# One slot block always, three conditional parts: the experts of a mixture-of-experts kernel cut anew

## The chip, the cores and the metric

The kernel runs on one core of a Trainium2 chip. The metric is the time of one execution on the device, in microseconds (us), as the median of several runs; a profile of one execution tells where it goes. The engines are TensorE (PE: matmuls, with a sequencer of its own, PEq, that reads the instructions; PEld is its loading of the stationary operand), VectorE (DVE), ScalarE (ACT), GpSimd (POOL), which here issues the gathers and scatters, and SyncE (SP), which issues the weights' transfers.

## What is computed

A decoder block for 512 tokens of width 1024: a state-space branch and a gated MLP branch, merged (the front of the kernel, 432 us), and then a mixture of experts, with which the change is concerned: each token goes to 4 of 32 experts, and each expert has a matrix of 1024 x 2048 for gate and up and one of 1024 x 1024 back.

```
logits = tok @ router_w + router_b
top_val, top_idx = lax.top_k(logits, 4); weights = softmax(top_val)
for e in range(32):                          # for the tokens that chose e
    gu = tok @ w_in[e] + b_in[e]             # 1024 -> 2048
    gate, up = min(gu[:, :1024], 7), clip(gu[:, 1024:], -7, 7)
    act = (up + 1) * (gate * sigmoid(1.702 * gate))
    out[tokens] += weight * (act @ w_out[e] + b_out[e])
x = x + gate2 * out; return rms_norm(x, final_g)
```

The inputs are fixed, and so is how many tokens come to each expert: between 12 and 159.

## The kernel before

**Slots.** An expert's tokens are put into slots, in steps of 32 (`SLOT`). Its weights are 12 tiles of 1 MB (8 `wi`, 4 `wo`), 384 in all, through a ring of 19 tiles in SBUF that SP's queue refills in the order of the experts, as far ahead as the ring lets it. The tokens' rows are gathered from DRAM by tables of slots (`tab0`, `tab1`, `tabp`) with an indirect DMA on POOL (`gather`, L1275), transposed on PE (L1298), and the results are added back into `acc` by an indirect DMA (`give`, L1383).

**Two shapes of block.** A block of 64 slots (`ab_up`, L1334, two halves u of 32 matmuls; `ab_out` and `ab_down`, L1343) puts 64 slots on the columns of the stationary operand and splits the 128 partitions of the result in 2. A block of 32 slots (`c_up`, L1366; `c_down`, L1376) splits them in 4, and takes as many matmuls as half a block of 64.

**What is unconditional.** In `expert(e)` a block of 64 slots always runs (tiles `xab`, PSUM tiles `pu` and `pd`, table `tab0`). Behind flat conditions, each an If on a flag that every engine has loaded from `nbt` (L1282), stand a single block of 32 (`single`, for 65 to 96 tokens and above 128) and a block of 64 more (`pair`, above 96). So an expert of up to 64 tokens takes two blocks of 32, one of 65 to 96 three, then four, then five.

**Order on PE.** It is the order of the code (PE is scheduled by hand): for each expert the flags' loads, the conditions of the gathers for e+2 (L1288, L1290; PE only steps past them), If single: up (L1434), If pair: up (L1436), the main block's up with the transposes of the next expert's rows between its halves, If single: down (L1445), If pair: down (L1447), the main block's down. All 32 experts are unrolled. A condition that is false makes an engine's sequencer jump over the rows of its body.

Of the kernel before, what the change touches and what calls it, by code (L numbers as in the profile page):

```python
# [29 lines left out]
SLOT = 32  # L30
# [11 lines left out]
def tile_hybrid_block(ctx: ExitStack, tc: tile.TileContext, x, c, ada_w, ada_b, norm1_g, w_in,  # L42
# [977 lines left out]
    reps = mc.tile([128, 5, 128], F32R, name="reps")  # L1020
    v.tensor_copy(reps[:, 0].rearrange("p (a b) -> p a b", a=2), ident[:, 0:64].unsqueeze(1).to_broadcast([128, 2, 64]))
# [3 lines left out]
    rep64, rep32 = [reps[:, 0]], [reps[:, 1 + j] for j in range(4)]  # L1025
# [106 lines left out]
    def positions(i, pps):  # L1132
        ns = slice(4 * i, 4 * i + 4)
        yield v.tensor_mul(pps_e, mk[:, i], pps[:, 0:32].unsqueeze(1).to_broadcast([128, 4, 32]))
        yield v.reduce_sum(pos[:, ns], pps_e, axis=mybir.AxisListType.X)
        yield one_hots(pos, 64, i)

    def later_hots(ch):

        v.tensor_scalar(pos2, pos, float(64 - 128 * ch), None, op0=OP.add)  # L1140
        for i in range(4):
            one_hots(pos2, 128, i)
# [52 lines left out]
    spread(slot_ps, 64, 1)  # L1195
    spread(slot_ps, 64, 2)
# [5 lines left out]
    spread(slot_ps, 64, 3)  # L1202
# [7 lines left out]
    tab0, tabp = [rt.tile([128, 1, 32, 3], I32, name=m) for m in ("tab0", "tabp")]  # L1210
    tab1 = rt.tile([128, 4, 32, 3], I32, name="tab1")
    tabl = dram.tile([18, 128, 96], I32, name="tabl")


    nbt = rt.tile([1, 97], I32, name="nbt")
    nbf = sm.tile([1, 97], F32, name="nbf")

    pair4 = rt.tile([128, 32], mybir.dt.uint8, name="pair4")
    def tables(t, n, reps, tab, mul, o, ps_, tile_):

        N = tab.shape[1]
        r = tile_("slt")[0:n]
        sc.activation(r, t[0:n, 0:96], AF.Copy)
        ps = ps_()
        for b, rep in enumerate(reps):
            pe.matmul(ps[:, 96 * b:96 * b + 96], rep[0:n], r, start=True, stop=True)
        pv = ps[:, 0:96 * N].rearrange("p (n v e) -> p n v e", n=N, v=3)
        iv, em = [tile_(n).rearrange("p (n e) -> p n e", e=32)[:, 0:N] for n in ("iv", "em")]
# [8 lines left out]
    def front_tile(n):  # L1237
        return sm.tile([128, 96], F32R, name=n) if n == "slt" else sm.tile([128, 64], F32, name=n)

    tables(slot_ps, 64, rep64, tab0, 2.0, 2, M, front_tile)  # L1240
# [6 lines left out]
    v.reduce_max(nbf[:, 96:97], nbf[:, 0:32], axis=mybir.AxisListType.X)  # L1247
    v.tensor_scalar(nbf[:, 64:96], cps[0:1, 0:32], 3.0 * SLOT + 0.5, None, op0=OP.is_gt)
    v.scalar_tensor_tensor(nbf[:, 32:64], cps[0:1, 0:32], 2.0 * SLOT + 0.5, nbf[:, 64:96], op0=OP.is_gt, op1=OP.subtract)
    v.scalar_tensor_tensor(nbf[:, 32:64], cps[0:1, 0:32], 4.0 * SLOT + 0.5, nbf[:, 32:64], op0=OP.is_gt, op1=OP.add)  # L1250
    v.tensor_copy(nbt, nbf)
    v.tensor_scalar(pair4, cps[:, 0:32], 3.0 * SLOT + 0.5, None, op0=OP.is_gt)
    later_hots(1)
    ordered.__exit__(None, None, None)
    xab = [rt.tile([128, 512], F32, name=f"xab{a}") for a in range(3)]
    xce = [rt.tile([128, 768], F32, name=f"xce{a}") for a in range(3)]
    gp.memset(xab[0], 0.0)
# [4 lines left out]
    pab = ctx.enter_context(tc.tile_pool(name="pab", bufs=1, space=PS, reuse_waits="tile"))  # L1262
    pcd = ctx.enter_context(tc.tile_pool(name="pcd", bufs=3, space=PS, reuse_waits="tile"))
# [15 lines left out]
    single, pair = {}, {}  # L1279

    def gather_first(e):
        single[e], pair[e] = [nc.values_load(nbt[0:1, o + e:o + e + 1], min_val=0, max_val=1) for o in (32, 64)]  # L1282
        gather(xab[e % 3], hrow2, tab0[:, 0, e, 0:1], 2)

    def gather_more(e):

        x_ = xce[e % 3]
        with tc.If(single[e] > 0):  # L1288
            gather(x_[:, 512:768], hrow4, tab1[:, 0, e, 0:1], 4)
        with tc.If(pair[e] > 0):  # L1290
# [287 lines left out]
```

## Time and profile before

| what | us |
|---|---|
| median of 3 runs | 1576.27 (1575.02 to 1578.70) |
| the profiled execution, its own time | 1573.51 |
| its span in the profile | 1571.9 |
| PE busy | 1397.8 (89%) |
| first expert's first up matmul | 432.5 |
| last expert's last matmul | 1544.1 |

The span is cut into the front (up to 432.5), the 32 experts (1111.6 us) and a tail of 27.8 us. "Idle before, releaser" in the profile's rows is the time for which an engine stood before the group of instructions, and what it waited for; PEq L1436 there means that PE's own sequencer came late, at the branch of line 1436.

### The profile page before, as it was taken

Reading aid. Unit: us, or ns where it says so; the run is one execution under the profiler, and the core shown is the slowest. Engines: PE = TensorE matmul, PEld = TensorE weight load, DVE = VectorE, ACT = ScalarE, POOL = GpSimd, SP = SyncE. Lnnn points to the kernel's source line nnn. Section 1 sums busy time; section 2 is a strip of 40 time slices with the busy share of each in tenths; the row PEclk is TensorE's granted clock in tenths of the full one; section 3 lists DMA queues with packets and bytes.
Section 4 is the critical chain, followed back from the end, with each engine's and each line's share of the span. In section 5 each row is a group of like instructions: output and inputs, shape, how many; then the busy total and the mean of one; then the engine's idle time right before and its main releaser. Section 6 shows DMA issues by size and latency. Waiting matters only on the chain. (4 is left out here: it accounts for less than half of the span.)

```text
span 1571.9 us, 21693 instructions
## 1 busy us (share of the span) xinstructions
PE 1397.8 (89%) x7671; PEld 643.2 (41%) x7672; DVE 519.3 (33%) x1095; ACT 345.4 (22%) x831; POOL 289.2 (18%) x204
## 2 busy tenths in 40 slices
PE   5889879969598889989999999998899999999992
PEld 3678757748432233323333333323233333333330
DVE  7868948893512111211111211111211111111114
ACT  3362313324321112111121112111121121211112
POOL 3643425350201010111010111101110211101001
PEclk9899979979699999999999999999999999999996
DMA  9353668383899999999997899989999999859953
GB/s 311 107 125 116 222 216 274 90 307 137 305 351 406 402 405 410 406 401 411 404 402 275 318 394 409 395 299 393 407 402 361 365 405 400 312 221 342 399 215 128
DMA packets 128915, 497.06 MB, mean 316 GB/s; under 512 B 23588, under 2 KB 31236, under 8 KB 95972
## 3 DMA queue, kind: packets, MB, share of 16 engines
q1 hardware_dynamic: 113844, 468.50, 76.3%
q0 software_dynamic: 11888, 20.84, 5.9%
q10 hardware_dynamic: 3008, 5.38, 1.0%
q8 instruction: 111, 1.82, 0.5%
q14 instruction: 64, 0.52, 0.1%
HBM read 476.75 MB, written 20.40 MB: 316 GB/s over the span
## 5 line engine op out<-in xcount | busy, mean ns | idle before, releaser
L1334 PE MATMUL pu<-wi,xab 128*64 128x512 f32 x2048 | 460.0, 602 | 1.8 <-issue 1.8
L1334 PEld LDWEIGHTS pu<-wi,xab 128*64 128x64 f32 x2048 | 144.8, 138 | 279.3 <-issue 269.1
L1343 PE MATMUL pd<-wo,aab 128*64 128x512 f32 x1024 | 233.8, 598 | 7.5 <-ACT aab L1306 7.3
L1304 ACT ACTIVATE xab<-pt,sh2c,g2c 128x64 f32<-128x64 f32 x304 | 93.8, 413 | 360.7 <-PE pt L1298 360.7
L1312 DVE TENSOR_SCALAR g<-pu 128x256 f32<-128x256 f32 x64 | 27.1, 423 | 405.3 <-PE pu L1334 401.2
L1343 PEld LDWEIGHTS pd<-wo,aab 128*64 128x64 f32 x1024 | 67.8, 136 | 129.1 <-issue 110.9
L1383 POOL DMA_INDIRECT acc<-yab,tab x32 | 50.7, 1585 | 361.4 <-DVE yab L1354 288.2
L175 POOL TENSOR_TENSOR wlo<-wraw,whi 128x1024 fp32r<-128x1024 f32 x34 | 93.0, 2738 | 128.0 <-ACT whi L174 114.7
L1275 POOL DMA_INDIRECT xab<-hrow,tab x32 | 33.6, 1051 | 375.7 <-PE pt L1298 373.1
L1366 PE MATMUL pc<-wi,xc 128*32 128x512 f32 x768 | 88.5, 608 | 9.6 <-DMA wi<-in_moe_w_in 6.8
L1354 DVE SCALAR_TENSOR_TENSOR yab<-pd,tab,gate2h 128x512 f32<-128x512 f32 x32 | 24.0, 751 | 199.9 <-PE pd L1343 199.9
L1313 ACT ACTIVATE s<-g 128x256 f32<-128x256 f32 x88 | 36.5, 415 | 222.2 <-DVE g L1312 220.6
L1334 PE MATMUL pc<-wi,xab 128*64 128x512 f32 x384 | 83.7, 594 | 1.0 <-ACT xab L1304 0.9
L403 PE MATMUL g<-hlo,whi 128*128 128x512 f32 x160 | 67.7, 423 | 7.1 <-DVE hlo L510 7.1
L403 PE MATMUL g<-hhi,whi 128*128 128x512 f32 x160 | 68.3, 427 | 2.7 <-ACT hhi L516 2.7
L1306 ACT ACTIVATE aab<-pt 128x256 f32<-128x256 f32 x64 | 24.5, 383 | 206.4 <-PE pt L1298 206.4
L1312 DVE TENSOR_SCALAR g<-pc 128x256 f32<-128x256 f32 x24 | 10.2, 424 | 170.4 <-PE pc L1366 96.6
L403 PE MATMUL g<-hhi,wlo 128*128 128x512 f32 x160 | 66.5, 415 | 0.0
L174 ACT ACTIVATE whi<-wraw 128x1024 fp32r<-128x1024 f32 x46 | 48.2, 1056 | 71.3 <-PE g L403 51.7
L354 DVE SCALAR_TENSOR_TENSOR adaw<-adaw,cT 128x1024 f32<-128x1024 f32 x28 | 54.4, 1944 | 0.8
L1298 PE MATMUL pt<-ident,act 128*128 128x128 f32 x176 | 36.3, 294 | 17.9 <-PEq L1447 10.4
L1298 PEld LDWEIGHTS pt<-ident,act 128*128 128x128 f32 x176 | 17.9, 141 | 80.9 <-issue 80.0
(446 smaller groups left out, 1644.8 us busy)
## 6 DMA issues: line engine op xcount, KB each, us to landing
wi<-in_moe_w_in SPq DMA_DIRECT2D x256, 1024.0 KB
wo<-in_moe_w_out SPq DMA_DIRECT2D x128, 1024.0 KB
adaw<-in_ada_w SPq DMA_DIRECT2D x16, 1024.0 KB
wraw<-in_w_in SPq DMA_DIRECT2D x12, 1024.0 KB
wraw<-in_ada_w SPq DMA_DIRECT2D x8, 1024.0 KB
wraw<-in_w_out SPq DMA_DIRECT2D x4, 1024.0 KB
xt<-in_x SPq DMA_DIRECT2D x4, 512.0 KB
wraw<-in_w_in SPq DMA_DIRECT2D x4, 512.0 KB
```

The lines of the kernel that those rows point to most:

```text
L174: sc.activation(dst_hi, src, AF.Copy)
L175: lo.tensor_sub(dst_lo, src, dst_hi)
L354: between.append(lambda k=k: v.scalar_tensor_tensor(a, w[k // 2][:, k % 2], cT[:, k:k + 1], a, op0=OP.mult, op1=OP.add))
L403: pe.matmul(P["ps"][m], l, r, start=(k == 0 and n == 0), stop=(k == 2 * P["n"] - 1 and n == 2))
L1298: pe.transpose(ps[:, 128 * j:128 * j + 128], src[:, 128 * j:128 * j + 128], ident)
L1304: sc.activation(t[:, o:o + w], ps[:, o:o + w], AF.Identity, scale=g2c[:, k:k + 1], bias=sh2c[:, k:k + 1])
L1312: v.tensor_scalar(g, p[:, 0:256], LIMIT, None, op0=OP.min)
L1313: sc.activation(sg, g, AF.Sigmoid, scale=ALPHA)
L1334: pe.matmul(p[u][64 * g:64 * g + 64, :].rearrange("p (a b) -> p a b", a=2), xT[:, k % 4, 64 * (k // 4):64 * (k // 4) + 64], wi[k][:, :, 51 ...
L1343: pe.matmul(p[64 * g:64 * g + 64, :], aT[:, k % 2, 16 * (k - k % 4):16 * (k - k % 4) + 64], wo[k // 2 + j][:, k % 2, 512 * g:512 * g + 512 ...
L1366: pe.matmul(p[32 * g:32 * g + 32, :].rearrange("p (a b) -> p a b", a=2), xT[:, k % 2, 32 * (k // 2):32 * (k // 2) + 32], wi[k][:, :, 256 * ...
L1383: gp.indirect_dma_start(out=rows_, out_offset=bass.IndirectOffsetOnAxis(ap=icol, axis=0), in_=y, in_offset=None, compute_op=OP.add)
```

## The change

The unconditional part of an expert becomes one block of 32 slots (`c_up` and `c_down`, PSUM tag `pm`, rows `xm`, table `tab0` for slots 0 to 31). Behind three flat Ifs stand a single block (33 to 64 tokens, and 97 to 128; `tab1`), a pair of 64 slots (above 64; `taba`) and a second pair (above 128; `tabb`). So an expert takes as many blocks of 32 as it needs, from one to five. The main block's up now stands behind the three conditional ups (but ahead of them for expert 0), and the next expert's transposes behind it. Each expert loads three flags. The gathers of conditional rows are issued one expert ahead instead of two, into two buffers (`xe`) instead of three. In the front, the first pass of one-hot tables goes to 96 slots instead of 64, two more tables are worked out on DVE there (`tab1` and `taba`), and two more small operations on the flags.

```diff
-    pair4 = rt.tile([128, 32], mybir.dt.uint8, name="pair4")
+    over3 = rt.tile([128, 32], mybir.dt.uint8, name="over3")
...
+    over = lambda n, dst, x_, op: v.scalar_tensor_tensor(dst, cps[0:1, 0:32], n * SLOT + 0.5, x_, op0=OP.is_gt, op1=op)
+    v.tensor_scalar(nbf[:, 64:96], cps[0:1, 0:32], 2.0 * SLOT + 0.5, None, op0=OP.is_gt)
+    v.tensor_scalar(nbf[:, 96:128], cps[0:1, 0:32], 4.0 * SLOT + 0.5, None, op0=OP.is_gt)
+    over(1.0, nbf[:, 32:64], nbf[:, 64:96], OP.subtract)
+    over(3.0, nbf[:, 32:64], nbf[:, 32:64], OP.add)
+    v.tensor_sub(nbf[:, 32:64], nbf[:, 32:64], nbf[:, 96:128])
     v.tensor_copy(nbt, nbf)
+    tables(slots, 96, rep32[1:2], tab1, 4.0, 0, M, front_tile)
+    tables(slots, 96, rep64[1:], taba, 2.0, 2, M, front_tile)
     later_hots(1)
...
     def gather_first(e):
-        single[e], pair[e] = [nc.values_load(nbt[0:1, o + e:o + e + 1], min_val=0, max_val=1) for o in (32, 64)]
-        gather(xab[e % 3], hrow2, tab0[:, 0, e, 0:1], 2)
+        flags[e] = [nc.values_load(nbt[0:1, o + e:o + e + 1], min_val=0, max_val=1) for o in (32, 64, 96)]
+        gather(xm[e % 3], hrow4, tab0[:, 0, e, 0:1], 4)
...
+    def pair_up(x_, wi, sel, n):
+        p, a_ = [PC(), PC()], acts(4, "actp", 2)
+        ab_up(transposed(x_, 4, "xab", 1, True), wi, sel, n, p)
+        return [swiglu(t, a) for t, a in zip(p, a_)]
+
+    def pair_down(a_, wo, sel, n, row):
+        lT = [transposed(t, 2, "ac", 4) for t in a_]
+        ab_out(PC(), lT[0], lT[1], wo, sel, n, row)
...
         if e + 2 < NE:
             gather_first(e + 2)
-            gather_more(e + 2)
-        act, last = acts(2, "act"), acts(3, "actc")
-        with tc.If(single[e] > 0):
-            c_up(transposed(x_[:, 512:768], 2, "xc", 2, True), wi, sel, n, last[2])
-        with tc.If(pair[e] > 0):
-            p = ab_up(transposed(x_[:, 0:512], 4, "xab", 2, True), wi, sel, n, [PC(), PC()])
...
-        nxt = []
-        p = ab_up(xT, wi, sel, n, [pab.tile([128, 512], F32, tag=f"pu{u}", name="pu") for u in range(2)],
-                  lambda: nxt.extend(start(e + 1) if e + 1 < NE else []))
...
+        if e and e + 1 < NE:
+            gather_more(e + 1)
+        (act,), (one,) = acts(1, "act"), acts(1, "actc")
+        ups = {}
+
+        def main_up():
+            c_up(xT, wi, sel, n, act, PM())
+
+        if e == 0:
+            main_up()
+        with tc.If(single > 0):
+            c_up(transposed(x_[:, 0:256], 2, "xm", 3, True), wi, sel, n, one)
+        with tc.If(pair > 0):
+            ups[0] = pair_up(x_[:, 256:768], wi, sel, n)
+        with tc.If(pair2 > 0):
+            ups[1] = pair_up(x_[:, 768:1280], wi, sel, n)
+        if e:
+            main_up()
+        nxt = start(e + 1) if e + 1 < NE else []
+        with tc.If(single > 0):
+            c_down(transposed(one, 2, "ac", 4), wo, sel, n, tab1[:, 0, e])
+        with tc.If(pair > 0):
+            pair_down(ups[0], wo, sel, n, taba[:, 0, e])
+        with tc.If(pair2 > 0):
+            pair_down(ups[1], wo, sel, n, tabb[:, 0, e])
+        c_down(transposed(act, 2, "am", 2), wo, sel, n, tab0[:, 0, e], PM())
```

On PE, the up part of one expert of the kernel before, from the first condition to the end of the main block's up (`pc` are the conditional blocks' PSUM tiles; "32x512 x32" is a block's matmuls, each of which the trace shows as two matmuls with two weight loads, and `xce` the gathered rows of the conditional blocks):

```order
L1434 COMPARE_AND_BRANCH
L1298 MATMUL pt<-ident,xce_3257 128x128 x2
L1366 MATMUL pc<-wi,xc 32x512 x32
L1434 UNCONDITIONAL_BRANCH x2
L1436 COMPARE_AND_BRANCH
L1298 MATMUL pt<-ident,xce_3257 128x128 x4
L1334 MATMUL pc<-wi,xab 64x512 x32
L1436 UNCONDITIONAL_BRANCH x2
L1334 MATMUL pu<-wi,xab 64x512 x16
L1298 MATMUL pt<-ident,xab_3252 128x128 x4
```

The same place in the changed kernel (line 1463 is the single's If, 1465 the pair's, 1467 the second pair's; `xe` holds the conditional rows, `xm` the main block's):

```order
L1463 COMPARE_AND_BRANCH
L1386 MATMUL pc<-wi,xm 32x512 x32
L1463 UNCONDITIONAL_BRANCH x2
L1465 COMPARE_AND_BRANCH
L1310 MATMUL pt<-ident,xe_3280 128x128 x4
L1344 MATMUL pc<-wi,xab 64x512 x32
L1465 UNCONDITIONAL_BRANCH x2
L1467 COMPARE_AND_BRANCH
L1467 UNCONDITIONAL_BRANCH x2
L1333 MATMUL pm<-bhl,sel 128x512
L1386 MATMUL pm<-wi,xm 32x512 x32
L1310 MATMUL pt<-ident,xm_3277 128x128 x2
```

A third conditional body, as long as the second, now stands between the loads and the main block's up, and what follows it is one block of 32 matmuls in the place of two halves of 16 in 64-slot form.

The down part of the changed kernel on the same engine, from the single's If (line 1472) past the pair's (1474) and the second pair's (1476) to the main block's down (`act` are the activations that are transposed):

```order
L1472 COMPARE_AND_BRANCH
L1396 MATMUL pc<-wo,ac 32x256 x32
L1474 COMPARE_AND_BRANCH
L1361 MATMUL pc<-wo,ac 64x512 x16
L1476 COMPARE_AND_BRANCH
L1310 MATMUL pt<-ident,act 128x128 x4
L1333 MATMUL pc<-bhl,sel 128x256 x2
L1476 UNCONDITIONAL_BRANCH x2
L1310 MATMUL pt<-ident,act 128x128 x2
L1333 MATMUL pm<-bhl,sel 128x256
L1396 MATMUL pm<-wo,am 32x256 x32
```

Here too a third condition with a body of 16 matmuls of 64x512 has come in, and the main block's down, 16 of 64x512 before, is 32 of 32x256.

## Rows read from the trace of the kernel before

**Rows 1.** The page: DMA share in 40 slices; the instruction queue's packets, MB.

```profile
DMA  9353668383899999999997899989999999859953
...
q8 instruction: 111, 1.82, 0.5%
```

**Rows 2.** Windows, experts 0 to 9 and 10 to 31.

```profile
core 0: us, PE busy (x) PEld busy (x) DVE busy (x) ACT busy (x) POOL busy (x), PEclk, DMA share, GB/s
432.50:739.70 307.20, 279.92 (x1481) 94.85 (x1480) 49.38 (x114) 51.64 (x152) 35.99 (x28) 0.97 1.01 399
739.70:1544.10 804.40, 763.80 (x4228) 266.44 (x4226) 136.39 (x317) 136.91 (x418) 90.08 (x67) 1.00 0.91 351
```

**Rows 3.** Windows, one expert of two, three, four and five blocks.

```profile
671.10:696.50 25.40, 23.65 (x111) 8.03 (x110) 4.38 (x10) 3.96 (x12) 3.91 (x3) 1.00 1.03 405
1419.90:1456.70 36.80, 35.43 (x244) 12.55 (x242) 6.46 (x15) 7.13 (x22) 3.14 (x2) 1.00 0.94 357
765.10:812.90 47.80, 46.53 (x219) 16.11 (x218) 8.06 (x19) 8.04 (x24) 4.25 (x3) 1.00 1.02 403
812.90:872.30 59.40, 58.27 (x351) 20.72 (x352) 10.15 (x24) 10.98 (x34) 5.76 (x4) 1.00 0.77 291
```

**Rows 4.** PE's groups, the single's and the pair's ups.

```profile
L1366 PE MATMUL pc<-wi,xc 128*32 128x512 f32 x768 | 88.5, 608 | 9.6 <-DMA wi<-in_moe_w_in 6.8 <-ACT xc L1304 2.8
L1334 PE MATMUL pc<-wi,xab 128*64 128x512 f32 x384 | 83.7, 594 | 1.0 <-ACT xab L1304 0.9
```

**Rows 5.** Timeline of PE in expert 28 (three blocks): start, length, work, idle before.

```profile
1420.76 7.07 PE L1366 MATMUL pc<-wi,xc 128*32 128x512 f32 x64 [0.23 <-ACT xc L1304]
...
1428.65 7.09 PE L1334 MATMUL pu<-wi,xab 128*64 128x512 f32 x32
...
1444.18 3.66 PE L1376 MATMUL pc<-wo,ac 128*32 128x256 f32 x64 [0.35 <-ACTq L1447]
...
1449.06 1.94 PE L1343 MATMUL pd<-wo,aab 128*64 128x512 f32 x8 [0.23 <-ACT aab L1306]
...
1451.30 5.37 PE L1343 MATMUL pd<-wo,aab 128*64 128x512 f32 x24
```

**Rows 6.** Timeline of PE after two conditions passed over, up and down.

```profile
671.72 0.70 PE L1321 MATMUL pu<-bhl,sel 128*128 128x512 f32 x2 [0.58 <-PEq L1436]
...
662.65 0.41 PE L1298 MATMUL pt<-ident,act 128*128 128x128 f32 x2 [0.73 <-PEq L1447]
```

**Rows 7.** Branches of the pair's conditions on PE's sequencer, ns min/median/max.

```profile
L1436 PEldq COMPARE_BRANCH  x38: 70/218/5188, 430.8 to 1519.6; - x38
...
L1447 PEldq COMPARE_BRANCH  x38: 70/213/437, 448.7 to 1535.0; - x38
```

**Rows 8.** Timeline of PE at the late entries of the main up.

```profile
580.67 0.70 PE L1321 MATMUL pu<-bhl,sel 128*128 128x512 f32 x2 [3.06 <-PEq L1436]
581.31 8.78 PE L1334 MATMUL pu<-wi,xab 128*64 128x512 f32 x32
...
1088.95 0.70 PE L1321 MATMUL pu<-bhl,sel 128*128 128x512 f32 x2 [3.43 <-PEq L1436]
1089.58 7.09 PE L1334 MATMUL pu<-wi,xab 128*64 128x512 f32 x32
```

**Rows 9.** Windows on the first half of the main up, behind two late entries.

```profile
581.30:590.00 8.70, 8.70 (x33) 2.61 (x32) 0.00 (x0) 0.00 (x0) 0.00 (x0) 0.80 1.05 389
...
1089.60:1096.70 7.10, 7.10 (x34) 2.29 (x34) 0.00 (x0) 0.00 (x0) 0.00 (x0) 1.00 1.04 381
```

**Rows 10.** Gathers of conditional rows on POOL (ns), and the gathers' landing.

```profile
L1275 POOL DMA_INDIRECT xce<-hrow,tab x12: 997/1075/1241, 486.0 to 1415.4; - x12
...
DMA to landing us min/median/max: 6.3/6.9/9.1
```

**Rows 11.** Timeline of DVE in the front: a table's first and last operation.

```profile
413.84 0.19 DVE L1229 TENSOR_SCALAR em<-m 128x32 f32<-128x32 f32 x1 [1.60 <-PE m L1226]
...
414.53 0.20 DVE L1235 TENSOR_TENSOR tab<-tab,m 128x32 f32<-128x32 f32 x1
```

More of the change, by code (lines that the diff above doesn't have):

```diff
@@ L1024, in tile_hybrid_block @@
                       ident[:, 32 * j:32 * j + 32].unsqueeze(1).to_broadcast([128, 4, 32]))
-    rep64, rep32 = [reps[:, 0]], [reps[:, 1 + j] for j in range(4)]
+    v.tensor_copy(reps[:, 5].rearrange("p (a b) -> p a b", a=2), ident[:, 0:64].unsqueeze(1).to_broadcast([128, 2, 64]))
+    rep64, rep32 = [reps[:, 5], reps[:, 0]], [reps[:, 1 + j] for j in range(4)]
     tok4 = sm.tile([128, 4], F32, name="tok4")
@@ L1237, in front_tile @@
     def front_tile(n):
-        return sm.tile([128, 96], F32R, name=n) if n == "slt" else sm.tile([128, 64], F32, name=n)
-    tables(slot_ps, 64, rep64, tab0, 2.0, 2, M, front_tile)
+        return sm.tile([128, 96], F32R, name=n) if n == "slt" else sm.tile([128, 32], F32, tag=n, name=n)
+    slots = sums(slot_ps, 96, front_tile)
+    tables(slots, 96, rep32[0:1], tab0, 4.0, 0, M, front_tile)
     cps = M()
@@ L1321, in biased, with acts, ab_up @@
         return pe.matmul(o, s_, bhl[:, n, cols_], start=first, stop=False)
-    def acts(n, tag):
-        return [mo.tile([128, 256], F32, tag=tag, bufs=n, name="act") for _ in range(n)]
-    def ab_up(xT, wi, sel, n, p, between=None):
+    def acts(n, tag, m=None):
+        return [mo.tile([128, 256], F32, tag=tag, bufs=n, name="act") for _ in range(m or n)]
+    def ab_up(xT, wi, sel, n, p):
         for u in range(2):
@@ L1330, in ab_up @@
         for k, u in [(k, u) for k in range(4) for u in range(2)] + [(k, u) for u in range(2) for k in range(4, 8)]:
-            if between and (k, u) == (4, 0):
-                between()
             for g in range(2):
@@ L1349, in ab_out @@
         ab_down(pd, aT0, 0, wo, (0, 1))
-        aT1 = aT1()
         ab_down(pd, aT0, 0, wo, (4, 5))
@@ L1359, in PC, with PM, c_up @@
         return pcd.tile([128, 512], F32, tag="pc", name="pc")
-    def c_up(xT, wi, sel, n, act):
-        p = PC()
+    def PM():
+        return pab.tile([128, 512], F32, tag="pm", name="pm")
+    def c_up(xT, wi, sel, n, act, p=None):
+        p = p or PC()
         biased(p, sel[:, 0], n, slice(0, 512))
@@ L1369, in c_up, with c_down @@
         return swiglu(p, act)
-    def c_down(aT, wo, sel, n, row):
-        p = PC()
+    def c_down(aT, wo, sel, n, row, p=None):
+        p = p or PC()
         biased(p[:, 0:256], sel[:, 0], n, slice(512, 768))
@@ L1403, in later_tables @@
         s_ = start(0) if ch == 1 else None
[L1404 to L1406 removed]
+        tab = mo.tile([128, 512], F32, tag="yab", bufs=2, name="tl")[:, 0:384].bitcast(I32)
+        tab = tab.rearrange("p (n e w) -> p n e w", n=4, w=3)
+        r = sums(t, 128, mo_tile)
+        tables(r, 128, rep32, tab, 4.0, 0, PT, mo_tile)
         if ch == 1:
[L1408 to L1411 removed]
+            tables(r, 128, rep64[0:1], tabb, 2.0, 2, PT, mo_tile)
+        gp.dma_start(tabl[4 * ch - 1:4 * ch + 3].rearrange("n p f -> p n f"), tab.rearrange("p n e w -> p n (e w)"))
+        return s_, tab
     ordered = tc.manual_schedule(engines={ET.PE})
     ordered.__enter__()
[L1415 to L1417 removed]
+    s_, tl = later_tables(1)
+    v.copy_predicated(tab1[:, 0], over3.unsqueeze(2).to_broadcast([128, 32, 3]), tl[:, 0])
+    most = nc.values_load(nbt[0:1, 128:129], min_val=0, max_val=NBMAX)
+    with tc.If(most > 7):
         for ch in (2, 3, 4):
```

103 lines of the change are left out of this document (40 added, 63 removed).

## The prediction, as it went on record

> **What bounds the kernel now.** I read the page first, then windows over the experts, PE's groups, PE's timeline within one expert, and last the branches. In the page the reader should see that DMA is full in most slices behind the front [rows 1]. The windows split that: to the end of expert 9 the queues are full (share 1.01), and PE works 280 of 307 us; from expert 10 on PE is busy 764 of 804 us and the queues are at 0.91 [rows 2]. So weights set the pace first, and PE afterwards. Second, an expert's time goes by its blocks: 25.4 us with up to two blocks of 32, 36.8 with three, 47.8 with four, 59.4 with five [rows 3]. There are 768/64 = 12 singles and 384/64 = 6 pairs [rows 4], which makes 17 experts of up to two blocks, 9 of three, 3 of four, 3 of five: 17 x 25.4 + 9 x 36.8 + 3 x 47.8 + 3 x 59.4 = 1085 us. The experts really take 1112; the other 27 us are waits for weights, late instructions and half-speed stretches behind them. How many of the 17 have one block only no trace shows; the reference's routing, counted on its inputs, gives 7 (experts 1, 2, 3, 5, 20, 23, 29) and 10 with two.
>
> Third, the late instructions. Two conditions passed over cost PE 0.58 us at the up and 0.73 at the down [rows 6]. The branch itself takes 0.2 us in the middle, but at the up's pair condition up to 5.19 us, at the down's never over 0.44 [rows 7]. A comparison of a register doesn't grow to 5 us; what it waits for is, I infer, the code behind it: the instruction queue brings 1.82 MB in 111 packets, 16.4 KB each [rows 1]. The difference between the places is the length of the jump. A single's up has 144 rows of instructions (64 matmuls, 64 weight loads, transposes, bias, semaphores, branches), a pair's up 150, the two downs 137 and 81. So a jump over 218 rows has always found its code there, one over up to 294 sometimes not. I take the middle, 256 rows, for a packet, and that PE's sequencer holds the packet it is in and asks for the next one when it enters it.
>
> **The change, part by part.**
>
> *Matmuls.* The main block's up falls from 2 x 7.09 to 7.07 us and its down from 1.94 + 5.37 to 3.66 [rows 5]: 10.8 us less. Back come one more passed condition at each end (some 0.2 us each) and a wait for the activations (four operations on DVE and ACT behind the last matmul, of which the first half's used to lie under the second half; I take 0.5 us, between 0 and 2). So a one-block expert needs 25.4 - 10.8 + 0.4 + 0.5 = 15.5 us. A single block more is 36.8 - 25.4 = 11.4 us and a pair 47.8 - 25.4 = 22.4 [rows 3], each less 0.5 for conditions no longer passed: 26.4, 37.4, 48.8 and 60 us for two to five blocks, where 25.4, 36.8, 47.8 and 59.4 stood. Ten experts lose 1 us, nine 0.6, six about 0.8, seven gain 9.9. In sum 1036: 49 us less than 1085 if nothing else waits.
>
> *Weights.* Experts 1, 2, 3 and 5 lie where the queues are full [rows 2]; their 40 us couldn't be had anyhow, since expert 9's last tiles come no sooner.
>
> *Code.* This is the term that decides. One expert's rows on PE, run or passed, are about 749 before (2.93 packets) and 1038 after (4.06; bodies of 144, 150, 152, 137, 81, 81 and the main block's 138 and 140). A one-block expert jumps over 446 rows at the up and 299 at the down, both beyond a packet; a two-block expert over 302 and 162. A packet's time F is at least 5.19 us [rows 7], and at most 25.4/2.93 = 8.7, the pace at which a two-block expert now gets through its packets; I take 5.5, near the row. Then I walk the rows of an expert: a packet can't be entered until F after the one before it. For one block: the jump of 446 rows takes 1 us, the main up 7.6, the jump of 299 about 1 and the down 5. If the first packet border lies at the expert's first row, the borders come at 0, 0.6, 4.6 and 9.2 us of undisturbed time; the second waits 4.9, the third 1.5, the fourth 0.9: 22.8 us. Borders 64, 128 and 192 rows later give 24.8, 23.9 and 21.9; the mean is 23.3, against 4.06 x 5.5 = 22.3 as the least. For two blocks (single up 8.3 us, jump 302 in 0.9, main up 7.8, down 4.5, jump 162 in 0.7, down 4) the four positions wait 1.5, 0.2, 5.3 and 6.6: 3.4 in the mean, 29.8. For three blocks no jump exceeds 152 rows and the walk gives 0.2 us: 37.6; for four and five nothing to 0.5. Bounds of this term: nothing (code always there), and F = 6.5 with 26.4 and 31.5 us.
>
> [...]
>
> *Clock.* [...] The walk has about 19 waits of over 3 us; three in four of them at 1.65 us make 23 us (bounds 0 and 31).
>
> *Small parts.* Two more tables at 0.9 us (five operations from 413.84 to 414.73 [rows 11]) and two flag operations stand on DVE ahead of the second one-hot pass: 2.2 us later for expert 0. The third flag's load and gather condition on PE's sequencer lie under its lead over PE; uncovered, 0.7 us an expert. The gathers are issued on POOL behind the previous expert's scatter, some 5 us into an expert; with 1.1 us and 6.9 to landing [rows 10] the conditional rows are there after 13 to 16 us, hidden under any expert of 22. Uncovered, 1 us in a few one-block experts. Issues of weights only follow PE.
>
> *Sum.* 7 x 23.3 + 10 x 29.8 + 9 x 37.6 + 3 x 48.8 + 3 x 60.3 = 1127; with the clock 1150, with the front's 2 us 1152, against 1112: +41 us. The weights no longer hold it up, since experts 0 to 9 would take 3 x 29.8 + 4 x 23.3 + 3 x 37.6 and their share of the clock, some 307 us as now. On the profiled 1573.5 that is 1614; the median lies 2.8 above this execution, so 1617. The walk leaves no room for waits at an expert's ends, and I go up to 1620.
>
> **Rivals.**
>
> *Code is always there in time* (chance 0.13). If F were under some 3.8 us (15.5/4.06), or two packets were held ahead, no jump would wait. For it: half of the branches at L1436 take 0.22 us or less, and none at L1447 over 0.44 [rows 7]. Against it: 5.19 us has been seen. Then experts 10 to 31 gain 3 x 9.9 less 7 x 1.0 and 12 x 0.7, that is 14 us; experts 0 to 9 gain the 7 us by which the main block's up behind the last tile is shorter; 2 us are lost in the front, and a few by gathers and by weights behind a short expert: about 1557 on the profiled execution and 1560 as a median, faster.
>
> *It evens out* (0.08). At F near 4.2 a one-block expert takes some 20 us and a two-block one 27.5; that gives back what the 14 + 7 us bring: 1576.
>
> *Longer waits* (0.13). F at 6.5 and the clock at half behind each wait: one-block experts 28, two-block 33, three-block 39: 196 + 330 + 351 + 148 + 184 = 1209, or +97: 1670. For it: the queues stay nearly full [rows 1], and F's upper bound is 8.7. Against it: the half-speed stretch failed to come once in the rows shown [rows 8].
>
> *The likeliest* (0.66): 1620, its own range 1585 to 1655.
>
> **How the numbers follow.** Faster is the first rival; same (within 0.2%, 3 us, about what a measurement of this kernel can tell) most of the second; slower the rest: 0.14, 0.06, 0.80. The range from 1564 to 1660 leaves out most of the first rival and of the third.
>
> **What would show it.** In the profile after: branches of the up's pair conditions at 3 to 6 us in nearly every one-block expert, and also at the down, where now none is over 0.44; more packets in the instruction queue, about 111 + 32 x 1.13 = 147; one-block experts of 21 to 28 us and two-block ones of 28 to 34; three-block experts within 2 us of 37.6; DMA share well under 1 also before 740 us; many stretches at a granted clock of 0.8 or less behind such waits. The prediction is wrong if the branches stay at 0.2 to 0.4 us, or if one-block experts come near 16 us.

## The result, and the profile after

The changed kernel takes 1684.72 us in the median (1681.11 to 1690.10, 4 runs), the kernel before in the same session 1575.64 us: ratio 1.069, 95% interval 1.0666 to 1.0714. It is slower, as forecast, but by 109 us where 44 were forecast, and outside the range. The profiled execution spans 1683.0 us, 111 more than before. The first up matmul comes 3.9 us later (436.5), the experts take 1219.7 us instead of 1111.6, and the tail is 1 us shorter.

The page of the changed kernel (busy time by engine, DMA share in 40 slices, the instruction queue's packets and MB):

```profile
PE 1362.1 (81%) x9935; PEld 654.8 (39%) x9936; DVE 514.5 (31%) x1093; ACT 359.3 (21%) x921; POOL 327.0 (19%) x229
...
DMA  9362757555499999999767899689995998856973
...
q8 instruction: 147, 2.41, 0.6%
```

and its windows over experts 0 to 9 and 10 to 31, then one expert of one, two, three, four and five blocks:

```profile
436.50:773.00 336.50, 252.15 (x2066) 92.57 (x2065) 43.04 (x101) 50.38 (x166) 41.22 (x31) 0.88 0.96 380
773.00:1656.20 883.20, 756.41 (x5906) 280.53 (x5906) 135.22 (x315) 150.92 (x492) 121.65 (x89) 0.96 0.82 315
1180.60:1210.70 30.10, 17.42 (x135) 6.01 (x134) 2.60 (x6) 2.94 (x10) 3.69 (x3) 0.72 1.03 405
1210.80:1245.20 34.40, 26.95 (x268) 10.24 (x268) 4.55 (x11) 5.90 (x20) 6.58 (x5) 0.90 1.02 398
1371.20:1410.90 39.70, 35.19 (x242) 12.80 (x242) 6.57 (x15) 6.91 (x22) 6.43 (x5) 1.00 0.93 371
803.60:853.10 49.50, 46.70 (x380) 17.52 (x376) 8.53 (x20) 9.75 (x32) 7.85 (x6) 1.00 0.80 312
853.10:917.20 64.10, 59.62 (x352) 21.48 (x350) 10.43 (x24) 10.76 (x34) 7.25 (x6) 0.97 0.59 214
```

Beside [rows 2] the reader sees PE doing less (1008.6 us busy in the experts instead of 1043.7) in a longer time, at a lower granted clock (0.88 and 0.96 instead of 0.97 and 1.00): PE stands idle for 211 us instead of 68. Beside [rows 3], the three-block expert shown takes 39.7 instead of 36.8 us, the four-block one 49.5 instead of 47.8, the five-block one 64.1 instead of 59.4. From the end of one main down to the next, the means over all experts of a size are 27.7, 31.9, 40.7, 49.5 and 64.1 us for one to five blocks; the one-block experts, which have 10.8 us less of matmuls, take longer than before (27.7 where the same seven took 26.4).

Where PE waits in an expert of one block (expert 20) and in one of two (expert 21), on its timeline:

```profile
1190.12 0.77 PE L1333 MATMUL pm<-bhl,sel 128*128 128x512 f32 x1 [9.48 <-PEq L1467]
1190.82 9.55 PE L1386 MATMUL pm<-wi,xm 128*32 128x512 f32 x64
...
1203.68 0.69 PE L1310 MATMUL pt<-ident,act 128*128 128x128 f32 x2 [2.94 <-ACTq L1476]
...
1204.84 5.94 PE L1396 MATMUL pm<-wo,am 128*32 128x256 f32 x64 [0.26 <-ACT am L1318]
...
1223.36 0.76 PE L1333 MATMUL pm<-bhl,sel 128*128 128x512 f32 x1 [3.75 <-PEq L1467]
1224.06 8.30 PE L1386 MATMUL pm<-wi,xm 128*32 128x512 f32 x64
...
1238.97 0.41 PE L1310 MATMUL pt<-ident,act 128*128 128x128 f32 x2 [1.82 <-DVEq L1474]
...
1239.85 5.35 PE L1396 MATMUL pm<-wo,am 128*32 128x256 f32 x64 [0.35 <-ACT am L1318]
```

The main up waits 9.48 us behind a jump over all three conditional ups, and 3.75 behind one over two of them. Both times the up that follows, 7.07 us at a granted clock of 1.00, takes 9.55 and 8.30 (granted 0.74 and 0.85), and the downs 5.94 and 5.35 instead of 3.66 (0.61 and 0.68). The branches themselves (lines 1465 and 1467, pair and second pair at the up; 1476, second pair at the down), and PE's longest waits over all experts:

```profile
L1465 PEldq COMPARE_BRANCH  x47: 70/176/4599, 451.9 to 1635.3; - x47
L1467 PEldq COMPARE_BRANCH  x35: 78/339/5650, 454.6 to 1638.0; - x35
L1476 PEldq COMPARE_BRANCH  x35: 73/217/3227, 461.2 to 1651.1; - x35
```

```profile
PE pm L1333 <- PEq L1467: 82.5, 28, 11.3
PE pt L1310 <- ACT xm L1316: 20.2, 18, 1.8
PE pt L1310 <- ACTq L1476: 18.9, 6, 3.4
PE pt L1310 <- PEq L1463: 17.1, 12, 1.7
PE pt L1310 <- PEq L1476: 12.4, 16, 4.2
...
PE pt L1310 <- DVEq L1474: 8.8, 6, 1.9
PE pc L1396 <- ACTq L1474: 8.6, 4, 2.6
PE pt L1310 <- ACTq L1472: 8.1, 3, 2.7
```

That a late branch waits for code can be read from the single packets in the trace. Each of the 20 branches of PE after 436 us that take over 0.7 us ends 1.3 to 1.5 us after a packet of the instruction queue has landed, and so do all 6 in the kernel before. In expert 20 packets land at 1182.92 and 1188.43, and the two late branches end at 1184.32 (L1465) and 1189.95 (L1467). Behind 16 of the 20 the next packet's transfer starts 3.0 to 3.6 us after the branch has ended, and it takes about 1.0: 3.3 + 1.0 + 1.4 = 5.7 us from one packet to the next.

So three places wait: the main up behind the jumps (82.5 us), the first transposes or matmuls of the downs (the rows at ACT xm, L1472, L1474 and L1476, together 77 us, 12.4 of them at PE's own branch L1476), and the first transposes of an expert (L1463, 17 us, and some 11 more under other names). Whatever the releaser, PE's idle time in the experts went from 26 to 82 us ahead of the main ups, from 30 to 95 ahead of the downs, and from 12 to 34 at the experts' starts. There is no wait for weights any more.

What stands ahead of the downs differs by expert. First ScalarE in expert 25 (three blocks), then VectorE in expert 21:

```profile
1395.70 0.38 ACT L1316 ACTIVATE xm<-pt,sh2c,g2c 128x32 f32<-128x32 f32 x1 [7.05 <-PE pt L1310]
...
1396.29 1.98 ACT L1316 ACTIVATE xm<-pt,sh2c,g2c 128x32 f32<-128x32 f32 x7
1398.12 0.42 ACT L1318 ACTIVATE ac<-pt 128x256 f32<-128x256 f32 x1
```

```profile
1237.21 0.48 DVE L1399 SCALAR_TENSOR_TENSOR yc<-pc,tab,gate2q 128x256 f32<-128x256 f32 x1 [4.36 <-PE pc L1396]
1237.62 0.41 DVE L1326 TENSOR_SCALAR u<-pm 128x256 f32<-128x256 f32 x1
...
1238.40 0.42 DVE L1328 SCALAR_TENSOR_TENSOR act<-u,g 128x256 f32<-128x256 f32 x1
```

In expert 25 the eight copies of the next expert's rows (`xm`) stand ahead of the first `ac` copy, which the pair's down needs, and PE waits 1.82 us there. In expert 21 it is no copy: the main block's activation (L1326 to L1328) stands on VectorE behind the result of the single's down (L1399), and the main down waits for it.

A last view, PE's groups, sizes the clock: 2048 main up matmuls (32 experts) and 2048 main down ones, and the pairs' downs (18 of them).

```profile
L1386 PE MATMUL pm<-wi,xm 128*32 128x512 f32 x2048 | 249.8, 643 | 0.0
...
L1396 PE MATMUL pm<-wo,am 128*32 128x256 f32 x2048 | 132.7, 416 | 11.1 <-ACT am L1318 10.8
L1361 PE MATMUL pc<-wo,ac 128*64 128x512 f32 x576 | 138.9, 639 | 0.1
```

At a granted clock of 1.00 these would be 32 x 7.07 = 226, 32 x 3.66 = 117 and 18 x 7.09 = 128 us: 50 us were lost there at 0.50, the lower of the two levels that the granted clock has in both traces, 24 of them in the main ups. In the experts the granted clock stood at that level in 29 stretches, 155 us in all; in the kernel before in 5, 23 us.

### The profile page after: what moved, and what is told of

Same layout as the page of the kernel before. It is cut to its first block, busy times and chain, and to the rows that moved or that the text cites. A ratio compares the mean times of both kernels' runs of the same rounds, so it can differ in the third digit from the quotient of the medians.

```text
span 1683.0 us, 27511 instructions
## 1 busy us (share of the span) xinstructions
PE 1362.1 (81%) x9935; PEld 654.8 (39%) x9936; DVE 514.5 (31%) x1093; ACT 359.3 (21%) x921; POOL 327.0 (19%) x229
## 4 chain that ended last, share of the span: by engine, by line
issue 26%; DMA 24%; another core or an unknown queue 1%; DVE 1%; POOLq 1%; PE 0%; POOL 0%; ACT 0%; ACTq 0%; DVEq 0%; SPq 0%
DMA acc<-yc,tab 14%; DMA acc<-yab,taba 5%; DMA acc<-yab,tabb 3%; DMA xe<-hrow,tab 2%; POOL xm L1284 0%; PE pm L1386 0%; POOLq L1292 0%; DMA fin<-acc 0%; DVE fs L1536 0%; DVE fs L1535 0%; DVE fin L1545 0%; POOLq L1403 0%; DVE fin L1552 0%; DVE fs L1537 0%
## 5 line engine op out<-in xcount | busy, mean ns | idle before, releaser
L1344 PE MATMUL pc<-wi,xab 128*64 128x512 f32 x1152 | 251.2, 594 | 2.0 <-ACT xab L1316 1.7
L1386 PE MATMUL pm<-wi,xm 128*32 128x512 f32 x2048 | 249.8, 643 | 0.0
L1316 ACT ACTIVATE xm<-pt,sh2c,g2c 128x32 f32<-128x32 f32 x360 | 104.6, 388 | 337.3 <-PE pt L1310 311.7
L1403 POOL DMA_INDIRECT acc<-yc,tab x45 | 73.0, 1623 | 505.1 <-DVE yc L1399 244.3
L1344 PEld LDWEIGHTS pc<-wi,xab 128*64 128x64 f32 x1152 | 81.2, 137 | 164.1 <-issue 149.0
L1396 PE MATMUL pm<-wo,am 128*32 128x256 f32 x2048 | 132.7, 416 | 11.1 <-ACT am L1318 10.8
L1361 PE MATMUL pc<-wo,ac 128*64 128x512 f32 x576 | 138.9, 639 | 0.1
L1386 PEld LDWEIGHTS pm<-wi,xm 128*32 128x32 f32 x2048 | 66.4, 117 | 164.2 <-issue 157.2
L1333 PE MATMUL pm<-bhl,sel 128*128 128x512 f32 x64 | 30.2, 471 | 88.7 <-PEq L1467 82.5
L1396 PEld LDWEIGHTS pm<-wo,am 128*32 128x32 f32 x2048 | 70.6, 119 | 64.3 <-ACT am L1318 17.1
L1386 PE MATMUL pc<-wi,xm 128*32 128x512 f32 x832 | 92.0, 594 | 3.5 <-ACT xm L1316 3.5
```

Of the source, the lines that this page charges most:

```text
L1316: sc.activation(t[:, o:o + w], ps[:, o:o + w], AF.Identity, scale=g2c[:, k:k + 1], bias=sh2c[:, k:k + 1])
L1344: pe.matmul(p[u][64 * g:64 * g + 64, :].rearrange("p (a b) -> p a b", a=2), xT[:, k % 4, 64 * (k // 4):64 * (k // 4) + 64], wi[k][:, :, 51 ...
L1361: pe.matmul(p[64 * g:64 * g + 64, :], aT[:, k % 2, 16 * (k - k % 4):16 * (k - k % 4) + 64], wo[k // 2 + j][:, k % 2, 512 * g:512 * g + 512 ...
L1386: pe.matmul(p[32 * g:32 * g + 32, :].rearrange("p (a b) -> p a b", a=2), xT[:, k % 2, 32 * (k // 2):32 * (k // 2) + 32], wi[k][:, :, 256 * ...
L1396: pe.matmul(p[32 * g:32 * g + 32, 0:256], aT[:, k % 2, 32 * (k // 2):32 * (k // 2) + 32], wo[k // 2][:, k % 2, 256 * g:256 * g + 256], sta ...
L1403: gp.indirect_dma_start(out=rows_, out_offset=bass.IndirectOffsetOnAxis(ap=icol, axis=0), in_=y, in_offset=None, compute_op=OP.add)
```

## Experiments

Three theories stood. *Code*: PE waits for rows of code behind long jumps. *Copies*: the eight copies of the next expert's rows, which the change had put between the main up and the downs on ScalarE, hold up the downs. *Sequencer*: three loads and three conditions at an expert's start are longer than PE's lead. All class means below are of the time from one expert's last main down matmul to the next's, read from each run's timeline.

**Code, by itself: a body that never runs, in the kernel before** (e4_before_pad, e5_before_pad_small). Both take the kernel before and add one condition at the up that is never true; its body has some 140 rows of PE in the one, one matmul in the other.

```diff
...
+        with tc.If(pair[e] > 1):
+            ab_up(xT, wi, sel, n, [PC(), PC()])
         nxt = []
```

```diff
...
+        with tc.If(pair[e] > 1):
+            biased(PC(), sel[:, 1], n, slice(0, 512))
         nxt = []
```

> The kernel before with a third condition at the up that is never true, with a body of 64 + 64 matmul and weight load rows on TensorE (about 140 rows) behind it. Theory 'code': the jump of the 17 experts that pass both conditions grows from 294 to some 435 rows; they wait 3 to 6 us more at the up, and half-speed stretches follow: 60 to 100 us more, about 1640 to 1675 us. Rival 'the condition itself' (the branch, the drain before it, the semaphores of the path passed): 0.2 to 0.4 us for each of 32 experts, about 10 us more, 1585 us.

> The kernel before with the same condition that is never true, but a body of one matmul. Theory 'code': the jump hardly grows, so only the condition's own price shows: 0.2 to 0.4 us for each of 32 experts, about 10 us more, 1585 us, far below the long body's time. Rival 'the condition itself': the same time as with the long body.

Measured: 1640.45 us with the long body (ratio 1.0391, 1.0327 to 1.0455), 1590.38 with the short one (1.0074, 1.0054 to 1.0094). Both came as the theory of code had it, the long body at the lower end of its range: the condition costs 12 us, 140 rows that never run cost another 50 (41 and 59 in the two runs of the long body). The 17 experts of up to two blocks rose from 25.9 us in the mean to 28.3 with the long body and 26.8 with the short one, so by less than the 3 to 6 us that were expected; the nine experts with a single alone rose as well (39.8 against 38.4). The new branch (ns, min/median/max), first long, then short, shows the wait itself:

```profile
L1440 PEldq COMPARE_BRANCH  x32: 208/399/3336, 435.9 to 1578.5; - x32
```

```profile
L1440 PEldq COMPARE_BRANCH  x32: 208/212/342, 435.6 to 1536.3; - x32
```

In e4 each branch of over 0.7 us ends 1.3 to 1.5 us after a packet has landed, as in the changed kernel. The instruction queue brings 129 packets with the long body and 112 with the short one: 17 more, as 32 x 138 rows at the prediction's 256 to a packet give.

**Code taken away again** (e10_no_pair2). The kernel e7 below without the second pair's bodies, so without the work of the slots from 128 on.

```diff
-        with tc.If(pair2 > 0):
-            ups[1] = pair_up(x_[:, 768:1280], wi, sel, n)
...
-        with tc.If(pair2 > 0):
-            pair_down(ups[1], wo, sel, n, tabb[:, 0, e])
```

> The kernel with fixed order and early rows (1655 us) without the second pair's ups and downs: 152 rows of code less at the up and 81 at the down of each expert. It leaves out the work of the slots from 128 on, in three experts of 32. Theory 'code': the jump of a one-block expert is 294 and 218 rows, that of a two-block expert 150 and 81, as in the kernel before: one-block experts 17 to 20 us instead of 25.9, two-block 27 to 28 instead of 32.6, five-block experts 38.5 as they now have three blocks: 7 x 7 + 10 x 5 + 3 x 23 = 168 us less, about 1487 us. Rival 'not the code': only the work left out goes, 3 x 23 and 0.3 us for two conditions less in each of the others, about 1570 us.

Measured: 1535.95 us (ratio 0.9742), 119 less than e7, between the two forecasts. One-block experts fell from 25.9 to 23.0 us, with 19.6 to 23.4 in six of them; two-block ones from 32.6 to 28.8, with 26.8 to 27.1 in five; the three experts that lost work went to 37.5. What the theory of code missed is the weights' queue: expert 3 took 32.0 and expert 24 took 37.1 us, with waits for weights of 7.3 and 5.8 us in them.

```profile
PE pt L1310 <- PEq L1465: 32.7, 16, 7.1
...
PE pc L1386 <- DMA wi<-in_moe_w_in: 10.3, 8, 2.2
```

Part of what the shorter code gives back is so taken by the weights. With three pairs of some 23 us, the work left out, it would stand at about 1605 us, still above the kernel before.

**Nested conditions** (e2_nested): one If on more than 32 tokens around the three, the second pair within the first.

```diff
...
+        with tc.If(nb[e] > 1):
+            with tc.If(single > 0):
+                c_up(transposed(x_[:, 0:256], 2, "xm", 3, True), wi, sel, n, one)
+            with tc.If(pair > 0):
+                ups[0] = pair_up(x_[:, 256:768], wi, sel, n)
+                with tc.If(nb[e] > 4):
+                    ups[1] = pair_up(x_[:, 768:1280], wi, sel, n)
...
```

> The changed kernel with its conditions nested: an outer If on more than 32 tokens around all three, the second pair inside the first pair's If; same bodies, so the same rows of code, and as many loaded flags. Theory 'each packet on the way': a wait comes for every packet of code in which a branch lies; one long jump lands in its target's packet at once, so a one-block expert waits for one packet per jump instead of up to two (5 to 6 us at the up instead of 7 to 11), 2 to 4 us at the up and up to 1 at the down less, and the passed conditions cost less: one-block experts 23 to 25 us instead of 27.7, two-block experts unchanged within 1 us: about 1655 us. Rival 'the code streams through whatever is jumped over': only the conditions' own price goes, 0.3 us each: about 1675 us.

Measured: 1721.72 us (ratio 1.0923, 1.0880 to 1.0967), slower than either theory. The one-block experts did go from 27.7 to 25.5 us, and the branch of their one jump waits up to 6.57 us:

```profile
L1464 PEldq COMPARE_BRANCH  x32: 65/70/6565, 445.3 to 1654.8; - x32
```

but all others lost (33.1, 42.2, 53.6, 64.5), at the downs: the edit had changed the order into which the scheduler puts ScalarE's work. In expert 15, for one, the single's `ac` copy stood ahead of all eight `xm` copies in the changed kernel and stands behind them here. That order hadn't been held still, so this run doesn't judge the total.

**Copies** (e1_rows_early, e6_by_hand, e7_by_hand_early). The first moves the next expert's transposes ahead of the main up again.

```diff
-        if e:
-            main_up()
-        nxt = start(e + 1) if e + 1 < NE else []
+        if e == 0:
+            nxt = start(e + 1)
+        else:
+            nxt = start(e + 1) if e + 1 < NE else []
+            main_up()
```

> The changed kernel with one edit: the next expert's transposes and the eight ScalarE copies behind them stand ahead of the main block's up again, so that these copies lie under its matmuls. Theory 'copies': in the changed kernel they stand on ScalarE between the main up and the activations of the conditional downs, and TensorE waits 1.8 us before the pair's down in three- and five-block experts and 2.6 us in two-block ones; those waits go, one-block experts gain about 1 us: 12 x 1.8 + 10 x 2 + 7 x 1, some 45 us less, about 1638 us. Theory 'code only': the time is lost behind the jumps over conditional code alone, which this edit doesn't touch: within 10 us of the changed kernel, 1675 to 1685 us.

Measured: 1710.40 us (ratio 1.0829), 26 more than the changed kernel: the expectation fell. The timeline of expert 25 (three blocks) shows why:

```profile
1412.06 0.63 PE L1310 MATMUL pt<-ident,act 128*128 128x128 f32 x4 [0.46 <-PEq L1474]
...
1413.01 7.09 PE L1361 MATMUL pc<-wo,ac 128*64 128x512 f32 x32
1423.13 0.66 PE L1310 MATMUL pt<-ident,act 128*128 128x128 f32 x2 [3.04 <-DVE act L1328]
...
1424.26 6.27 PE L1396 MATMUL pm<-wo,am 128*32 128x256 f32 x64 [0.26 <-ACT am L1318]
```

The wait ahead of the pair's down is gone, but one of 3.04 us stands ahead of the main down, and the down behind it takes 6.27 us instead of 3.66. The scheduler had put the main block's swiglu behind the conditional downs on ScalarE and VectorE. Two more runs keep both engines to the order of the code, with the copies late (e6) and early (e7):

```diff
+    by_hand = tc.manual_schedule(engines={ET.DVE, ET.Activation})
+    by_hand.__enter__()
     for e in range(NE):
         s_ = expert(e, *s_)
+    by_hand.__exit__(None, None, None)
```

> The changed kernel with ScalarE and VectorE kept to the order of the code in the expert loop (TensorE already is): the main block's activation first, then the eight copies of the next expert's rows, then the conditional downs' activations. In the run with the rows early the scheduler had moved the main block's swiglu behind the conditional downs on both engines, which that edit didn't mean. This run is the control for the next: the copies still stand ahead of the downs' activations. Both theories: within 15 us of the changed kernel, 1670 to 1700 us.

> The same fixed order, and the next expert's transposes and copies ahead of the main block's up. Theory 'copies' (a wait of 1.8 to 2.6 us at the downs comes from the eight copies and their place on ScalarE): one-block experts 25 us, two-block 28 to 30, three-block 38 to 39, five-block 61 to 62; about 60 us less than the changed kernel, 1610 to 1640 us. Rival 'code only': the waits at the downs are code as well, and nothing changes: 1675 to 1690 us.

Measured: e6 1727.53 us (ratio 1.0961, 1.0921 to 1.1000), e7 1654.87 (1.0487, 1.0450 to 1.0524). Both fell outside their forecasts: e6 was to stay within 15 us of the changed kernel and came 43 above it, e7 came 15 above its range. With the order held still, the place of the transposes and their copies is worth 73 us between e6 and e7. PE's idle time ahead of the downs is 118 us in e6 and 64 in e7, where the changed kernel has 95. The class means go from 28.7, 33.2, 41.8, 53.0 and 65.0 us to 25.9, 32.6, 38.7, 50.1 and 61.9. The wait ahead of the pair's down in three-block experts, first e6, then e7:

```profile
957.52 0.66 PE L1310 MATMUL pt<-ident,act 128*128 128x128 f32 x4 [2.89 <-ACTq L1472]
```

```profile
1378.29 0.41 PE L1310 MATMUL pt<-ident,act 128*128 128x128 f32 x2 [0.46 <-PEq L1474]
```

Against the changed kernel itself, where the scheduler had put the copies partly behind the main activation, early copies in a fixed order give 30 us, and this run can't tell the place of the copies from the order of VectorE. What is left in e7 ahead of the main down of a one-block expert is the main block's own activation, 2.1 us in each of the seven:

```profile
PE pt L1310 <- DVEq L1474: 14.6, 7, 2.1
```

Two-block experts didn't reach the 28 to 30 us expected: their wait behind the jump remains.

**Sequencer** (e8_flags_mid, e12_one_load_more).

```diff
-        if e + 2 < NE:
-            gather_first(e + 2)
-        if e and e + 1 < NE:
-            gather_more(e + 1)
         (act,), (one,) = acts(1, "act"), acts(1, "actc")
...
+        if e + 2 < NE:
+            gather_first(e + 2)
+        if e and e + 1 < NE:
+            gather_more(e + 1)
         if e:
             main_up()
```

> The changed kernel with one edit: the three flags' loads and the gathers' conditions of an expert stand behind its conditional ups instead of at its start. Theory 'sequencer late at the start' (three loads and three conditions take TensorE's sequencer 2 us, its lead in the main down is 1.4 us): the idle time of 0.9 to 1.7 us ahead of the first transposes in experts of two and more blocks goes to 0.2 to 0.5; 25 x 0.9, some 20 us less: about 1662 us. Rival 'it only moves': the loads then hold up the main up behind the jump or the conditional matmuls, and the time stays within 5 us of the changed kernel.

Measured: 1731.43 us (ratio 1.0985): 47 more, far from both forecasts. The wait at the start does fall (1.43 to 0.56 us in a three-block expert), but the main up then waits 2.33:

```profile
1139.04 0.63 PE L1310 MATMUL pt<-ident,xe 128*128 128x128 f32 x4 [0.56 <-PEq L1459]
...
1156.45 0.50 PE L1333 MATMUL pm<-bhl,sel 128*128 128x512 f32 x1 [2.33 <-issue]
```

The second pair's condition is passed over just ahead. That it leaves nothing queued on PE under which the loads could lie is how I read these rows.

```diff
+        more[e] = nc.values_load(nbt[0:1, e:e + 1], min_val=0, max_val=NBMAX)
         gather(xm[e % 3], hrow4, tab0[:, 0, e, 0:1], 4)
```

> The changed kernel with a fourth flag load per expert, whose value nothing uses. Theory 'sequencer late at the start': TensorE waits 0.4 us longer ahead of the first transposes of the 25 experts with a conditional block, and behind the jump of the others: some 10 to 13 us more than the changed kernel, 1695 us. Rival 'hidden under the lead': no change.

Measured: 1689.31 us (ratio 1.0731, 1.0705 to 1.0757), 5 more than the changed kernel with overlapping intervals, and the class means are the same within 0.2 us. The waits at the experts' starts (L1463 and its other names) go from 28 to 33 us between the two traces, where 10 to 13 more were expected; a cost of the load in the total is not shown.

**All together, and nested on a fixed order** (e9_all, e11_nested_early): e7 with nested conditions, in e9 also with the flags behind the ups.

> The fixed order, early rows, flags behind the conditional ups, and the nested conditions in one kernel. If the four effects add: one-block experts 22 us, two-block 27.5, three-block 37.7, four 49, five 61: 7 x 22 + 10 x 27.5 + 9 x 37.7 + 3 x 49 + 3 x 61 = 1098 us for the experts, 122 less than the changed kernel's 1220, so about 1562 us, level with the kernel before or a little faster. If code is the bound (4.06 packets at 5.9 us, 24 us at the least): one-block 25, two-block 30: about 1610 us.

> Fixed order, early rows and the nested conditions, flags at the expert's start. If nesting takes away the second wait of a one-block expert's jump (24 us instead of 25.9) and costs nothing else: 7 x 2 + 10 x 0.5, about 1636 us. Rival: two waits become one, but a two-block expert's jump now lands beyond the packet that was asked for, and waits a whole fetch of 5.9 us where it waited 3.5: one-block experts 2 us less, two-block ones up to 2 us more, 1655 us.

Measured: e9 1670.95 us (ratio 1.0608), e11 1651.47 (1.0475, 1.0455 to 1.0495). The effects don't add: e9 pays for its flags as e8 did. In e11 the one-block experts come to 23.9 us, all between 23.0 and 24.7, near the 24 us that 4.06 packets at 5.9 us allow (the longest wait at L1467 in e2 is 5.88); two-block ones take 31.5. Its total is that of e7 within the intervals: three-block experts, 40.6 us in the mean, gave it back, one of them with 49.1.

**Nested conditions in the kernel before** (e13_before_nested at both ends, e14_before_down_nested, e15_before_up_nested), the only edits here that might beat it. The up's part:

```diff
-        with tc.If(single[e] > 0):
-            c_up(transposed(x_[:, 512:768], 2, "xc", 2, True), wi, sel, n, last[2])
-        with tc.If(pair[e] > 0):
...
+        with tc.If(nb[e] > 2):
+            with tc.If(single[e] > 0):
+                c_up(transposed(x_[:, 512:768], 2, "xc", 2, True), wi, sel, n, last[2])
+            with tc.If(nb[e] > 3):
```

> The kernel before with its single and pair conditions nested in one on more than 64 tokens, at the up and the down; two loads as before. Theory: 17 experts pass one condition instead of two at each end, 0.3 us each, 17 x 0.6 = 10 us less; the jump of 294 rows now and then lands in a packet not asked for and waits up to 5.9 us, in 2 or 3 of 17, as in the kernel before: about 1567 us. Rival: the jump is no cheaper in one piece, and the other experts pay a branch more: 1576 to 1585 us.

> The kernel before with the conditions nested at the down alone, where the jump has 218 rows. The kernel nested at both ends had most two-block experts at 24.3 instead of 25.3 us, but three- and five-block experts with 6 us more here and there, and ended level. Theory 'a long jump in one piece lands beyond the packet asked for': the outliers come from the up's 294 rows, so this kernel keeps half the gain, 17 x 0.5 less 9 x 0.3, and has none of them: about 1570 us. Rival 'where the packets' borders fall in the code': any new row shifts them, outliers of 3 to 6 us come and go with it, and the time is level again, 1576 to 1582 us.

> The same with the conditions nested at the up alone (294 rows). Theory 'a long jump in one piece': two or three experts of 17 wait 6 us, level with the kernel before or slower, 1576 to 1582 us. Rival 'where the borders fall': as for the other, level, with other experts late.

Measured: 1582.04 us (ratio 1.0027, 1.0014 to 1.0040), 1579.40 (1.0010, 0.9997 to 1.0023) and 1582.63 (1.0027, 1.0012 to 1.0041). None beats the kernel before. In e13 ten of the 17 experts of up to two blocks take 24.3 to 24.7 instead of 25.3 us, but the first expert starts 4.3 us later and some others are 2 to 6 us late. The theory that the up's long jump in one piece makes the late ones fell: e14 nests only the down, and yet six of the 17 take 27.3 to 29.0 us, at the up, which it left as it was; e15, which nests the up, has six as well. In all three each late branch ends 1.1 to 1.5 us after an instruction packet has landed. That they come and go with where the packets' borders fall in the code fits this, but no border's place in the code was read.

## Why the prediction went the right way and missed the size

*Right: what decides.* The code behind the jumps. The queue brings the 147 packets that were forecast, 36 more, as 32 x (1038 - 749) rows give; the up's branches wait up to 5.65 us, one at the down 3.23, where none was over 0.44 before [rows 7]; each late branch ends 1.3 to 1.5 us after a packet has landed, and the 5.7 us from packet to packet are near the 5.5 that the walk took; and e4 against e5 shows the price of rows that never run without any other change. That the next packet is asked for when one is entered was the author's assumption; the 3.0 to 3.6 us from the end of a late branch to the next transfer fit it, and how many packets the sequencer holds was not shown. The weights did stop being the bound (no wait for them in the experts), and came back as soon as the code was shorter (10.3 us at the single's ups in e10).

*Right in size, in part by luck: the walk.* Waits of 7.8 us for a one-block and 3.4 for a two-block expert make 89 us; the row at L1467 has 82.5 at the up alone, with the conditions' own 0.6 us each in it. But they stand elsewhere: seven one-block experts wait 58 us there, 8.3 each, two-block ones 23. The waits that the walk put into straight rows don't show (L1386 has 0.0 us of idle before it), and at the down only two branches are late (3.23 and 2.13 us).

*Failed: the step "clock".* It was 23 us with a bound of 31; the three groups above lost 50. No run shows its 1.65 us as the price of a wait: in [rows 8] 3.06 us of idle cost 1.69 and 3.43 us nothing, and here the main ups behind 9.48 and 3.75 us lost 2.48 and 1.23. The walk counted waits of 3 us and more, at the main ups for the most part, and there 24 us is what was lost. In the rows, the downs run slow as well (5.94 and 5.35 us, at 0.61 and 0.68), after waits of 2.94 and 1.82 us that came soon after a longer one. Part of this may be a result of the next point: each late down adds a wait, and the two shown ran at the lower clock.

*Failed: the wait for the activations at the downs, 0.5 us, and the copies, which had no term.* "Small parts" speaks of loads, gathers and tables. That `start(e + 1)` moved from between the halves of the up to behind it was told as a change and given no price. It puts eight copies (some 2.3 us) on ScalarE behind the main up, and in most experts the scheduler let a down wait for them, or for VectorE's work on another down. In six of the seven one-block experts the main down waits 2.9 to 3.4 us (the row at ACTq L1476); with the copies early it waits 2.1 (e7). So the activations alone cost four times the 0.5 there, and about 1 us is left for the copies. All in all PE's idle time ahead of the downs grew by 65 us. Three- and five-block experts, in which the walk had next to no waits, took 3.1 and 3.8 us more than forecast, 39 us of the 93 by which the experts' 1219.7 exceeds 1127; the next point has a share in that. How the 65 us divide between copies, VectorE's order, activations and PE's own conditions no run shows: the 73 us between e6 and e7 are those of two other orders, and against the changed kernel e7 gains 30.

*Failed: "lie under its lead over PE".* The first transposes of an expert wait 0.9 to 1.7 us in nearly all with a conditional block, 28 us in all (the row at L1463, with 6.5 and 4.7 us that the profile puts down to PE's own last matmul and to no releaser). The loads do lie under the main down: the last of the three ends 0.2 to 0.8 us before it does in each of experts 1 to 29. The four conditions behind them (L1298, L1300, L1302, L1463) don't; in expert 25 they run from 1370.64 to 1372.09, and the down ends at 1371.15. A fourth load (e12) added some 5 us, within overlapping intervals. The front's 3.9 us against 2.2 is not settled; e13 shows that such a start moves by 4 us with another edit in the experts alone.

*The sum, the signs and the rival.* By the prediction's own rule (0.5 us less for each condition no longer passed) four and five blocks come to 48.3 and 59.3 us instead of 48.8 and 60, 4 us of the sum; nothing turns on it. Two signs didn't come: three-block experts took 40.7 us in the mean, and the DMA share to 773 us was 0.96. The rival of longer waits (1670) came nearest, with 28, 33 and 39 us for one to three blocks, in part for its reason: its clock at half behind each wait is nearer to what was lost, but its F of 6.5 is not what the changed kernel shows, where the longest branch took 5.65.

## What to carry to other kernels

Rows of code that are jumped over aren't free (some 140 that never run cost 50 us between e5 and e4): count the instructions between a condition and its end per engine, and compare jumps with what the instruction queue brings in one packet and how long a late branch in the trace takes; a packet that lands just ahead of such a branch's end (1.3 to 1.5 us here) is the sign of it. When a block of work moves, list what each engine, also a lightly used one, now does between the last matmul of one phase and the first of the next, and hold that engine's order still before judging an edit: e1 and e2 were decided by what the scheduler did in reply. A saving of matmuls on PE is worth only what remains after the waits that it uncovers and the lower clock behind them: here one-block experts had 10.8 us less of matmuls and took 27.7 us instead of 26.4.

## What the hardware showed that was not expected

Conditions passed over in one jump wait once (up to 6.57 us in e2, and 7.01 in e11, where two packets land within the one wait), three passed one behind the other up to twice: in expert 1 the branches at L1465 and L1467 take 4.60 and 5.58 us, each ends 1.4 us after a packet has landed, and the main up waits 11.3. So each branch on the way waited for its own code. And code that is jumped over is fetched all the same: e4's body, which never runs, brings 17 packets more than e5's (129 against 112), and the nested kernel e11 has 147, as many as the changed one. And the granted clock fell (0.73 from 1238.9 to 1245.2) after an idle of only 1.82 us at the down that followed a wait of 3.75 us some 15 us earlier, while [rows 8] had one of 3.43 us without any effect; what the chip makes its choice by isn't settled here.
